# Diagonal blocks loaded group by group behind their stores, and the inverses of a scan's first groups stored in pieces of their own

## The chip, the core and the metric

The kernel runs on one core of one Trainium2 chip. The core has a matrix engine (PE, with its weight loads shown as PEld), a vector engine (DVE), a scalar engine (ACT), GpSimd (POOL), and SyncE (SP), which here does nothing but issue DMAs, in the order of its program. The metric is the time of one execution on the device in microseconds (us). A result is the median of several executions.

## What is computed

One layer of a hybrid encoder on x of 2048 rows and 1024 columns, in float32: RMSNorm, one combined input projection, then two groups of heads side by side, an output projection and the residual. One group is windowed attention (8 query heads, window 128). The other, with which the change is concerned, is a gated DeltaNet of 4 heads of width 128, scanned over the rows forward and backward. Cut to what matters, for one head and one direction, with the rows in chunks:

```python
g = jnp.cumsum(g, axis=-1)
decay = jnp.exp(jnp.where(incl, g[..., :, None] - g[..., None, :], -jnp.inf))
m = jnp.where(strict, jnp.einsum('bhncd,bhnsd->bhncs', k_beta, k) * decay, 0.0)
t_inv = triangular_solve(eye + m, eye, lower=True, unit_diagonal=True)
...
def step(state, inp):                      # one chunk after the other
    v_new = u_i - w_i @ state              # u, w = t_inv applied to v, k
    o = (q_i * exp(g_i)) @ state + a_i @ v_new
    state = state * exp(g_last) + k_dec.T @ v_new
```

Each chunk needs the inverse of a unit triangular matrix before its step of the scan, and the steps of a direction depend on each other through the state.

## The kernel before

The kernel uses chunks of 128 rows: 16 chunks a head and direction, in four groups of four (`c4` = 0 to 3). Phase A (`phase_a`) does norm, projections and attention. Phase B (`phase_b`) has four parts for each DeltaNet head `h`:

- `pre_front(h)`: for each group in the order FRONT = (1, 2, 0, 3) it loads k and q (L621), v (L623) and the decays (L631), multiplies k by k and q (tile `gh`, L661), forms the matrices `ma` for both directions (`d` = 0 and 1, L670), and stores the 128x128 matrices of the group to DRAM (`m_d<-ma`, L675: two DMAs a group, one a direction, 256 KB each, eight a head).
- `pre_back(h)`: it loads the 32x32 diagonal blocks out of `m_d`. A row of padding makes the four blocks of a matrix lie at equal distances, so that one strided DMA takes 64 of them, in pieces of 128 bytes: `L0` for direction 0 (L697) and the upper 64 partitions of `L` for direction 1 (L698), 256 KB each. DVE transposes the blocks of direction 0 into the lower half of `L` with one copy (L700). 31 steps on DVE (`tm` L705 and `X` L709, for all 128 blocks at once) then turn the identity in `X` (loaded in L699) into the inverses. One DMA stores all of `X` to DRAM (`x_d<-X`, L710, 512 KB). For each of four groups `hi`, two DMAs of 64 KB bring the inverses back in another layout (`xc<-x_d`, L718: the group `c4 = hi` of direction 0 and `c4 = 3 - hi` of direction 1), DVE transposes them (L719), POOL copies them into block matrices (`iv`, L724, L726 and L728, and `ma`, L745), and five rounds of matmuls (`pi`, L733) build the inverse of the whole 128x128 matrix.
- `scan(h)`: 16 steps, each for both directions: PE products `pk`, `py` and `po` (L773, L782, L784, L791, L800), scalings on ACT and DVE, and a load of k and q for the step (`kqc<-kq_d`, L771, four buffers a direction). Step `i` of the scan needs the inverses of group `hi = i // 4`, so `hi = 0` lets it begin.
- `post(h)`: norm and gate of the output (`jko` on ACT, `sso` on POOL, L829), stored as `mix_dn` (L843).

The calls stand in the order `pre_front(0)`, the attention half of the output projection (`out_sw`, tiles `pcs`, `xrs`), `pre_back(0)`, then `scan(h)`, `pre_front(h+1)`, `pre_back(h+1)` for `h` = 0, 1, 2, then `scan(3)` and the other half of the output projection (`out_dn`, tiles `pcd`). The engines do not run in that order. `set_order` (the planner) takes all instructions with their dependences and plans a start for each with costs of its own, forward and backward in turns, and then fixes the order on every engine by the plan. So work of head `h+1` is laid into the scan of head `h`. Two of its rules are used below: it counts an issue on SP as 500 ns, and it takes what waits for a DMA to be free 2400 ns plus bytes at 300 GB/s after the end of the issue:

```python
LAG = {"PE": 205, "DVE": 140, "Activation": 160, "Pool": 120, "SP": 2400}
...
            move[k] = a.ap[0][1] * size(a) * 4 / 300
```

Once planned, the order is fixed: an instruction that waits holds up all behind it on its engine, on SP too. A tile with one buffer (`L0`, `L`, `X`) can be written for the next head only when the last use of it for this head has ended; that also holds in the plan.

Of the kernel before, what the change touches and what calls it, by code (L numbers as in the profile page):

```python
# [7 lines left out]
F32 = mybir.dt.float32  # L8
# [7 lines left out]
P = 128  # L16
# [3 lines left out]
NCH = 16  # L20
# [496 lines left out]
def phase_b(ctx, tc, t, ident, consts, hp, mix_dn, mix_sw, kq_d, v_d, zdn_d, zsw_d, dp, out):  # L517
    nc = tc.nc
    V, A, G, T = nc.vector, nc.scalar, nc.gpsimd, nc.tensor
    dma = nc.sync.dma_start  # L520

    def pool(name, bufs=1, stack=ctx, **kw):
        return stack.enter_context(tc.tile_pool(name=name, bufs=bufs, reuse_waits="tile", **kw))
# [58 lines left out]
    qp = pool("qp", stack=pre_stack)  # L582
# [13 lines left out]
    def ma_tile(h, p):  # L596
        tag = f"ma{FREED[p] if h > 1 else p}"
        return hd[h % 2].tile([P, 4, 4, P], F32, tag=tag, name=f"ma{h}_{p}", bufs=1)

    def kv_tile(kind, h, n, name):  # L600
        p, slot = ((0, n), (1, n), (2, n) if n < 2 else (0, n - 2), (0, 2 + n) if n < 2 else (1, n - 2))[h]
        return (hd[p] if p < 2 else qp).tile([P, 4, P], F32, tag=f"{kind}{slot}", name=name, bufs=1)

    def pre_front(h):
        H = {}
        ssk = hp.tile([P, NCH], F32, tag="ssk", name=f"ssk{h}", bufs=1)
        nk = hp.tile([P, NCH], F32, tag="nk", name=f"nk{h}", bufs=1)
        bp = hp.tile([P, 2, NCH], F32, tag="bp", name=f"bp{h}")
        ssq = H["ssq"] = hp.tile([P, NCH], F32, tag="ssq", name=f"ssq{h}", bufs=3)
        ck = H["ck"] = hp.tile([P, 2, NCH], F32, tag="ck", name=f"ck{h}", bufs=3)  # L610
        ks = H["ks"] = {}
        vs = H["vs"] = {}
        mp = {}
        ma = H["ma"] = {}
        m_d = dp.tile([2, NCH, 4 * (32 * P + 32)], F32, tag="m_d", name=f"m_d{h}", bufs=2)
        x_d = dp.tile([2, NCH, P, 32], F32, tag="x_d", name=f"x_d{h}", bufs=2)
        for n, c4 in enumerate(FRONT):
            s4 = slice(4 * c4, 4 * c4 + 4)
            cs = slice(c4 * 512, (c4 + 1) * 512)
            kq = q1.tile([P, 2, 512], F32, tag="kq", name=f"kq{h}_{c4}", bufs=2)  # L620
            dma(kq, kq_d[h][:, :, cs])  # L621
            vt = q1.tile([P, 512], F32, tag="vt", name=f"vt{h}_{c4}", bufs=2)
            dma(vt, v_d[h][:, cs])  # L623
            gms = []
            for d in range(2):
                gm = q1.tile([P, 4, P], F32, tag="gm", name=f"dc{h}_{c4}_{d}", bufs=4)
                if h < NDEC:
                    dma(gm.rearrange("p c i -> p (c i)"), dec_d[h, d][c4])
                else:
                    src = gr_d[d].rearrange("(c h) i -> c h i", h=4)[s4, h]  # L630
                    dma(gm, src.partition_broadcast(P))  # L631
                    G.tensor_tensor(gm, gm, dmask[:, d : d + 1].to_broadcast([P, 4, P]), ALU.add)
                gms.append(gm)
                p = 3 - c4 if d else c4
                if p not in mp:
                    mp[p] = ma_tile(h, p)
                ma[d, c4] = mp[p][:, :, 1 - d :: 2]
            for j, ss in ((0, ssk), (1, ssq)):
                tr = ps_t.tile([P, 4, P], F32, tag="tr", name=f"tr{h}_{c4}_{j}")
                for c in range(4):  # L640
                    T.transpose(tr[:, c], kq[:, j, c * P : (c + 1) * P], ident)
                if j == 0:
                    ks[c4] = kv_tile("ks", h, n, f"ks{h}_{c4}")
                    A.activation(ks[c4], tr, AF.Copy)
                for c in range(4):
                    cc = 4 * c4 + c
                    src = ks[c4] if j == 0 else tr
                    jk = q1.tile([P, P], F32, tag="jk", name=f"jk{h}_{c4}_{j}_{c}", bufs=3)
                    A.activation(jk, src[:, c], AF.Square, accum_out=ss[:, cc : cc + 1])
            V.tensor_scalar(ssk[:, s4], ssk[:, s4], EPS, None, ALU.add)  # L650
            G.tensor_tensor(nk[:, s4], ssk[:, s4], pw[:, 0, :4], ALU.pow)
            V.reciprocal(ssk[:, s4], ssk[:, s4])
            V.tensor_tensor(
                bp[:, :, s4], beta[:, s4, h :: 4].rearrange("p c d -> p d c"),
                ssk[:, s4].unsqueeze(1).to_broadcast([P, 2, 4]), ALU.mult,
            )
            for c2 in range(2):
                gh = ps_g.tile([P, 2, 2, P], F32, tag="gh", name=f"gh{h}_{c4}_{c2}")
                for k in range(2):
                    c = 2 * c2 + k  # L660
                    T.matmul(  # L661
                        gh[:, k], kq[:, 0, c * P : (c + 1) * P], kq[:, :, c * P : (c + 1) * P], start=True, stop=True
                    )
                for k in range(2):
                    c = 2 * c2 + k
                    cc = 4 * c4 + c
                    for d in range(2):
                        if h >= NDEC:
                            A.activation(gms[d][:, c], gms[d][:, c], AF.Exp, bias=ngc[:, d, cc, h : h + 1])
                        V.scalar_tensor_tensor(  # L670
                            ma[d, c4][:, c], gh[:, k], bp[:, d, cc : cc + 1],
                            gms[d][:, c : c + 1].to_broadcast([P, 2, P]), ALU.mult, ALU.mult,
                        )
            for d in range(2):
                dma(m_d[d, s4, : P * P].rearrange("u (i j) -> i u j", j=P), ma[d, c4][:, :, 0])  # L675
            tr = ps_t.tile([P, 4, P], F32, tag="tr", name=f"trv{h}_{c4}")
            for c in range(4):
                T.transpose(tr[:, c], vt[:, c * P : (c + 1) * P], ident)
            vs[c4] = kv_tile("vs", h, n, f"vs{h}_{c4}")
            for c in range(4):  # L680
                cc = 4 * c4 + c
                A.activation(vs[c4][:, c], tr[:, c], AF.Copy, scale=nk[:, cc : cc + 1])
        for d in range(2):
            V.tensor_tensor(ck[:, d], bp[:, d], ekd[:, d, :, h], ALU.mult)

        H["solve"] = m_d, x_d, mp
        return H

    def pre_back(h, H):
        ma = H["ma"]  # L690
        m_d, x_d, mp = H["solve"]
        L0 = qp.tile([64, 32, 32], F32, tag="L0", name=f"L0{h}")
        L = qp.tile([P, 32, 32], F32, tag="L", name=f"L{h}")
        X = qp.tile([P, 32, 32], F32, tag="X", name=f"X{h}")
        lv = [m_d[d].rearrange("u (p y) -> (u p) y", p=4)[:, : 32 * P] for d in range(2)]
        lv = [a.rearrange("q (r x) -> q r x", x=P)[:, :, :32] for a in lv]
        dma(L0, lv[0])  # L697
        dma(L[64:128], lv[1])  # L698
        dma(X, t["eye32"].partition_broadcast(P))  # L699
        V.tensor_copy(L[0:64], L0.rearrange("p r c -> p c r"))  # L700
        for c in range(31):
            n = 31 - c
            tm = qp.tile([P, 256], F32, tag="tm", name=f"tm{h}_{c}")
            tv = tm[:, : n * (c + 1)].rearrange("p (r k) -> p r k", k=c + 1)
            XE.tensor_tensor(  # L705
                tv, L[:, c + 1 :, c : c + 1].to_broadcast([P, n, c + 1]),
                X[:, c : c + 1, 0 : c + 1].to_broadcast([P, n, c + 1]), ALU.mult,
            )
            XE.tensor_tensor(X[:, c + 1 :, 0 : c + 1], X[:, c + 1 :, 0 : c + 1], tv, ALU.subtract)  # L709
        dma(x_d.rearrange("d u (p r) c -> (d u p) (r c)", p=4), X.rearrange("p r c -> p (r c)"))  # L710
        for hi in range(4):
            e1, p2, e2, e3 = (z[hi % len(z)] for z in zts)
            m = mp[hi]
# [1 line left out]
            for d, c4 in ((0, hi), (1, 3 - hi)):  # L715
                xc = qp.tile([P, 4, 32], F32, tag="xc", name=f"xc{h}_{d}_{c4}", bufs=4)
                xt = qp.tile([P, 4, 32], F32, tag="xt", name=f"xt{h}_{d}_{c4}", bufs=4)
                dma(xc, x_d[d, 4 * c4 : 4 * c4 + 4].rearrange("u i c -> i u c"))  # L718
                V.transpose(xt.rearrange("p u c -> p (u c)"), xc.rearrange("p u c -> p (u c)"))  # L719
                x0[d], x1[d] = (xc, xt) if d == 0 else (xt, xc)  # L720
            g = qp.tile([P, 4, P], F32, tag="g", name=f"g{h}_{hi}", bufs=2)
# [111 lines left out]
    def post_rows(h, oa, so, c4):  # L833
# [9 lines left out]
        dma(mix_dn[h, :, c4 * 512 : (c4 + 1) * 512], zt)  # L843

    H = pre_front(0)
    with tc.using_default_side("right"):
        with ExitStack() as sw:
# [4 lines left out]
            )  # L852
        hd[1] = pool("hd1")
    pre_back(0, H)
    for h in range(3):
        scan(h, H)
        H = pre_front(h + 1)
        pre_back(h + 1, H)
# [365 lines left out]
```

## Time and profile before

| | |
|---|---|
| median of 3 runs | 1340.53 us (1336.61 to 1341.32) |
| profiled execution, its own time | 1339.74 us |
| span of its instructions | 1338.0 us, mean granted PE clock 0.979 |
| busy, of the span | PE 1258.0 us, DVE 885.6, ACT 711.3, POOL 484.4 |
| DMA | 201.16 MB, mean 150 GB/s |
| issues of `m_d` stores and `L` loads | 32 of 256 KB, 8 of 256 KB |
| issues of `x_d` stores and `xc` loads | 4 of 512 KB, 32 of 64 KB |

The span runs from the first to the last instruction of the profiled execution, and 1.7 us of that execution's time lie around it. In a row of the timeline stand start, duration, engine (SPq is SyncE's instruction queue), line, operation, output and input tiles, and, in brackets, how long the engine had been idle before and what ended the wait. A row of the stretches has their length, then the busy time of each engine with its count of instructions, the granted PE clock, the mean busy share of the 16 DMA engines, and GB/s. A row of the DMA issues ends with the size of one and the median time from issue to landing. The chain of waits is the chain of work that ended last, followed back from the last instruction.

### The profile page before, as it was taken

How to read it: one execution, taken by the hardware profiler on the slowest of the kernel's cores; microseconds unless marked ns; L12 is line 12 of the kernel's file. 1: busy time of each engine (PE TensorE's matmuls, PEld its weight loads, DVE VectorE, ACT ScalarE, POOL GpSimd, SP SyncE). 2: the span in 40 equal slices, each digit the busy share in tenths (PEclk: the TensorE clock that was granted, in tenths of full speed). 3: DMA queues.
4: the chain of work that ended last, by engine and by line, in shares of the span. 5: the costliest groups of instructions: out<-in, count | busy, mean ns of one | idle time of the engine just before them, and what ended most of it. 6: DMA issues, size and time to landing. Idle time of an engine off the chain costs nothing.

```text
span 1338.0 us, 22553 instructions
## 1 busy us (share of the span) xinstructions
PE 1258.0 (94%) x7162; PEld 1072.9 (80%) x7162; DVE 885.6 (66%) x2250; ACT 711.3 (53%) x2105; POOL 484.4 (36%) x868
## 2 busy tenths in 40 slices
PE   5999999999999999999999899998979879898998
PEld 4998878788998888888888687778868769788776
DVE  4423387773632399999987899666885877846433
ACT  5422264332433467666667877229868766466310
POOL 1223032100021235755786755228238155170000
PEclk8999999999999999999999999999979989989999
DMA  7442345244443533222334757968567274333776
GB/s 235 135 140 78 104 161 171 73 135 135 148 121 114 163 102 109 72 93 83 96 120 130 249 185 226 291 209 217 144 184 207 84 212 104 94 104 106 233 241 209
DMA packets 219686, 201.16 MB, mean 150 GB/s; under 512 B 48304, under 2 KB 170800, under 8 KB 219568
## 3 DMA queue, kind: packets, MB, share of 16 engines
q1 hardware_dynamic: 219568, 199.73, 48.8%
q8 instruction: 57, 0.93, 0.3%
q14 instruction: 61, 0.50, 0.1%
HBM read 134.59 MB, written 65.08 MB: 149 GB/s over the span
## 4 chain that ended last, share of the span: by engine, by line
PE 72%; DVE 9%; DMA 5%; ACT 5%; POOL 5%; issue 3%; SPq 0%; DVEq 0%; POOLq 0%; ACTq 0%
PE pf_c L186 6%; PE pf_c L187 6%; PE pf_c L188 5%; PE pf_z L186 4%; PE pf_z L187 4%; PE pf_z L188 4%; PE pi L733 4%; PE pt L360 2%; PE pq_q L197 2%; PE pq_q L199 2%; PE pq_q L198 2%; PE pcd L559 2%; PE pcd L560 2%; PE pcd L558 2%; PE pcs L558 2%
## 5 line engine op out<-in xcount | busy, mean ns | idle before, releaser
L237 DVE SCALAR_TENSOR_TENSOR acc<-pf_c,cw,acc 128x512 f32<-128x512 f32 (+1 forms) x192 | 140.0, 745 | 22.7 <-ACT acc L233 20.9
L186 PE MATMUL pf_c<-xhi,wh_c 128*128 128x512 f32 x384 | 149.3, 401 | 1.9 <-DVE acc L237 1.1
L187 PE MATMUL pf_c<-xlo,wh_c 128*128 128x512 f32 x384 | 150.4, 401 | 0.0
L188 PE MATMUL pf_c<-xhi,wl_c 128*128 128x512 f32 x384 | 148.4, 400 | 0.0
L186 PE MATMUL pf_z<-xhi,wh_z 128*128 128x512 f32 x256 | 91.6, 400 | 0.1
L355 POOL TENSOR_SCALAR pr<-pr,st 128x384 f32<-128x384 f32 (+1 forms) x128 | 83.5, 670 | 22.5 <-DVE st L353 19.0
L187 PE MATMUL pf_z<-xlo,wh_z 128*128 128x512 f32 x256 | 91.0, 397 | 0.0
L346 ACT ACTIVATE pr<-pr,st 128x384 f32<-128x384 f32 (+1 forms) x128 | 76.2, 598 | 27.3 <-DVE st L345 26.7
L188 PE MATMUL pf_z<-xhi,wl_z 128*128 128x512 f32 x256 | 90.3, 396 | 0.0
L186 PEld LDWEIGHTS pf_c<-xhi,wh_c 128*128 128x128 f32 x384 | 72.3, 189 | 17.5 <-DVE acc L237 1.9
L188 PEld LDWEIGHTS pf_c<-xhi,wl_c 128*128 128x128 f32 x384 | 72.0, 188 | 14.6
L187 PEld LDWEIGHTS pf_c<-xlo,wh_c 128*128 128x128 f32 x384 | 72.3, 188 | 13.9
L341 DVE CUSTOM_DVE_ANT_0 pr<-s,mask,sink 128x384 f32<-128x384 f32 (+1 forms) x128 | 72.6, 594 | 6.0 <-PE pt L360 2.5
L360 PE MATMUL pt<-ident,pr 128*128 128x128 f32 x368 | 72.8, 276 | 3.3 <-ACT q L323 1.4
L364 ACT ACTIVATE ph<-pt 128x512 fp32r<-128x512 f32 x92 | 53.4, 594 | 40.2 <-PE pt L360 37.3
L365 DVE TENSOR_TENSOR pl<-pt,ph 128x512 fp32r<-128x512 f32 x92 | 62.5, 684 | 9.1 <-ACT ph L364 7.9
L670 DVE SCALAR_TENSOR_TENSOR ma<-gh,bp,dc 128x256 f32<-128x256 f32 x128 | 56.1, 476 | 17.7 <-PE gh L661 10.0
L787 ACT ACTIVATE yk<-py,ck 128x128 f32<-128x128 f32 x120 | 44.0, 367 | 40.4 <-PE py L782 39.1
L360 PEld LDWEIGHTS pt<-ident,pr 128*128 128x128 f32 x368 | 48.6, 141 | 19.2 <-POOL pr L355 4.8
L178 DVE TENSOR_TENSOR wl_c<-ws_c,wh_c 128x512 fp32r<-128x512 f32 x48 | 36.6, 765 | 37.0 <-ACT wh_c L177 24.7
L197 PE MATMUL pq_q<-wh_q,xhi 128*128 128x256 f32 x256 | 58.5, 284 | 0.8 <-ACT sgq L256 0.8
L561 DVE TENSOR_TENSOR xrd<-xrd,pcd 128x512 f32<-128x512 f32 x32 | 20.9, 684 | 55.5 <-PE pcd L560 55.5
(250 smaller groups left out, 3769.9 us busy)
## 6 DMA issues: line engine op xcount, KB each, us to landing
kqc<-kq_d SPq DMA_DIRECT2D x120, 128.0 KB, 2.5
ws_c<-wt SPq DMA_DIRECT2D x48, 256.0 KB, 3.5
xr<-x SPq DMA_DIRECT2D x16, 512.0 KB, 6.0
ws_z<-wt SPq DMA_DIRECT2D x32, 256.0 KB, 3.4
kq<-kq_d SPq DMA_DIRECT2D x16, 512.0 KB, 4.9
xrs<-x SPq DMA_DIRECT2D x32, 256.0 KB, 3.4
part<-xrs SPq DMA_DIRECT2D x32, 256.0 KB, 3.4
m_d<-ma SPq DMA_DIRECT2D x32, 256.0 KB, 4.9
```

The source lines that it names most:

```text
L186: T.matmul(ps, hi[:, k, cs], xhi[b][:, k], start=(k == 0), stop=False)
L187: T.matmul(ps, hi[:, k, cs], xlo[b][:, k], start=False, stop=False)
L188: T.matmul(ps, lo[:, k, cs], xhi[b][:, k], start=False, stop=(k == KC - 1))
L197: T.matmul(ps[:, :n], xh, hi[:, k, :n], start=(k == 0), stop=False)
L237: V.scalar_tensor_tensor(av, ps[:, lo:], cw[:, i, k : k + 1], av, ALU.mult, ALU.add)
L341: V.tensor_tensor_reduce(pr[j][:, :n], ps[:, :n], mask[:, lo * P : hi * P], 1.0, sink[:, hh : hh + 1], ALU.add, ALU.max, accum_out=mx[:, j ...
L346: A.activation(pr[j][:, :n], pr[j][:, :n], AF.Exp, bias=nm[:, j : j + 1], accum_out=den[:, j : j + 1])
L355: G.tensor_scalar(pr[j][:, :n], pr[j][:, :n], den[:, j : j + 1], 1.0, ALU.mult, ALU.mult)
L360: T.transpose(pt[:, j], pr[j][:, (kb - lo) * P : (kb - lo + 1) * P], ident)
L365: V.tensor_tensor(pl, ptf, ph.bitcast(F32), ALU.subtract)
L558: T.matmul(ps, mh[:, k], wh[:, k, ns], start=(k == 0), stop=False)
L670: V.scalar_tensor_tensor(ma[d, c4][:, c], gh[:, k], bp[:, d, cc : cc + 1], gms[d][:, c : c + 1].to_broadcast([P, 2, P]), ALU.mult, ALU.mult,)
```

## The change

`L0` and `L` are now created in `pre_front`, and `m_d` becomes a tile of one group. Right behind the two stores of a group, two DMAs load that group's diagonal blocks, 16 partitions each (64 KB): eight loads a head in place of two. `x_d` is split into three tiles, and the store of `X` into three DMAs: partitions 0 to 15 (direction 0, group 0), 112 to 127 (direction 1, group 3), which together are all that `hi = 0` reads, and then the other 96. The loads `xc` read from the tile that holds their group. The arithmetic is the same.

```diff
@@ pre_front
-        m_d = dp.tile([2, NCH, 4 * (32 * P + 32)], F32, tag="m_d", name=f"m_d{h}", bufs=2)
-        x_d = dp.tile([2, NCH, P, 32], F32, tag="x_d", name=f"x_d{h}", bufs=2)
+        L0 = qp.tile([64, 32, 32], F32, tag="L0", name=f"L0{h}")
+        L = qp.tile([P, 32, 32], F32, tag="L", name=f"L{h}")
+        x_d = [dp.tile([4 * n, P, 32], F32, tag=f"x_d{j}", name=f"x_d{h}_{j}", bufs=2) for j, n in enumerate((1, 1, 6))]
         for n, c4 in enumerate(FRONT):
...
+            m_d = dp.tile([2, 4, 4 * (32 * P + 32)], F32, tag=f"m_d{n}", name=f"m_d{h}_{c4}", bufs=2)
             for d in range(2):
-                dma(m_d[d, s4, : P * P].rearrange("u (i j) -> i u j", j=P), ma[d, c4][:, :, 0])
+                dma(m_d[d, :, : P * P].rearrange("u (i j) -> i u j", j=P), ma[d, c4][:, :, 0])
+            for d in range(2):
+                lv = m_d[d].rearrange("u (p y) -> (u p) y", p=4)[:, : 32 * P]
+                lo = 64 * d + 16 * c4
+                dma((L if d else L0)[lo : lo + 16], lv.rearrange("q (r x) -> q r x", x=P)[:, :, :32])
@@ pre_back
-        L0 = qp.tile([64, 32, 32], F32, tag="L0", name=f"L0{h}")
-        L = qp.tile([P, 32, 32], F32, tag="L", name=f"L{h}")
         X = qp.tile([P, 32, 32], F32, tag="X", name=f"X{h}")
-        lv = [m_d[d].rearrange("u (p y) -> (u p) y", p=4)[:, : 32 * P] for d in range(2)]
-        lv = [a.rearrange("q (r x) -> q r x", x=P)[:, :, :32] for a in lv]
-        dma(L0, lv[0])
-        dma(L[64:128], lv[1])
...
-        dma(x_d.rearrange("d u (p r) c -> (d u p) (r c)", p=4), X.rearrange("p r c -> p (r c)"))
+        for a, lo, hi in zip(x_d, (0, 112, 16), (16, 128, 112)):
+            dma(a.rearrange("u (p r) c -> (u p) (r c)", p=4), X[lo:hi].rearrange("p r c -> p (r c)"))
...
-                dma(xc, x_d[d, 4 * c4 : 4 * c4 + 4].rearrange("u i c -> i u c"))
+                lo = 4 * (3 * d + c4 - 1 + d)
+                dma(xc, (x_d[2][lo : lo + 4] if hi else x_d[d]).rearrange("u i c -> i u c"))
```

More of the change, by code (lines that the diff above doesn't have):

```diff
@@ L684, in pre_front @@
             V.tensor_tensor(ck[:, d], bp[:, d], ekd[:, d, :, h], ALU.mult)
-        H["solve"] = m_d, x_d, mp
+        H["solve"] = L0, L, x_d, mp
         return H
@@ L690, in pre_back @@
         ma = H["ma"]
-        m_d, x_d, mp = H["solve"]
-        L0 = qp.tile([64, 32, 32], F32, tag="L0", name=f"L0{h}")
-        L = qp.tile([P, 32, 32], F32, tag="L", name=f"L{h}")
+        L0, L, x_d, mp = H["solve"]
         X = qp.tile([P, 32, 32], F32, tag="X", name=f"X{h}")
-        lv = [m_d[d].rearrange("u (p y) -> (u p) y", p=4)[:, : 32 * P] for d in range(2)]
-        lv = [a.rearrange("q (r x) -> q r x", x=P)[:, :, :32] for a in lv]
-        dma(L0, lv[0])
-        dma(L[64:128], lv[1])
         dma(X, t["eye32"].partition_broadcast(P))
```

## The prediction, as put on record before the result

> **What bounds the kernel now.** I read the page first: the busy shares and the chain of waits by engine.
>
> ```profile
> span 1338.0 us, 22553 instructions
> PE 1258.0 (94%) x7162; PEld 1072.9 (80%) x7162; DVE 885.6 (66%) x2250; ACT 711.3 (53%) x2105; POOL 484.4 (36%) x868
> PE 72%; DVE 9%; DMA 5%; ACT 5%; POOL 5%; issue 3%; SPq 0%; DVEq 0%; POOLq 0%; ACTq 0%
> ```
>
> PE is busy for 1258.0 of 1338.0 us and carries 72% of the chain. So the change, which touches no matmul, can win only where PE stands idle, and only in the part where diagonal blocks are solved. The stretches of that part say how much there is:
>
> ```profile
> 855.00:890.00 35.00, 33.14 (x143) 26.29 (x142) 30.62 (x80) 3.17 (x5) 0.00 (x0) 1.00 0.87 292
> 890.00:905.00 15.00, 11.56 (x64) 9.71 (x63) 4.80 (x14) 7.18 (x31) 9.39 (x31) 0.89 0.50 133
> 905.00:950.00 45.00, 42.44 (x320) 38.93 (x319) 30.04 (x95) 41.49 (x179) 32.26 (x66) 1.00 0.84 216
> 950.00:990.00 40.00, 35.14 (x234) 30.49 (x234) 38.13 (x141) 26.13 (x117) 5.32 (x5) 0.91 0.44 125
> 990.00:1010.00 20.00, 15.27 (x86) 13.10 (x86) 11.14 (x33) 16.70 (x72) 15.16 (x35) 0.74 0.97 261
> 1010.00:1055.00 45.00, 43.69 (x349) 40.84 (x349) 32.88 (x107) 36.20 (x138) 26.93 (x61) 1.00 0.52 139
> 1055.00:1090.00 35.00, 26.00 (x152) 21.93 (x152) 29.61 (x106) 21.60 (x107) 9.22 (x8) 0.90 0.60 179
> 1090.00:1120.00 30.00, 25.27 (x176) 22.24 (x175) 16.47 (x48) 20.97 (x80) 23.61 (x69) 0.94 0.63 154
> 1120.00:1160.00 40.00, 35.05 (x271) 32.48 (x270) 35.91 (x129) 24.82 (x94) 9.58 (x20) 0.98 0.23 64
> 1160.00:1176.00 16.00, 13.01 (x74) 10.89 (x73) 8.90 (x32) 5.80 (x28) 5.44 (x19) 0.82 0.59 168
> 1176.00:1240.00 64.00, 59.16 (x455) 55.30 (x453) 35.88 (x111) 44.12 (x156) 23.09 (x66) 0.98 0.36 102
> ```
>
> Length less the first busy number, added up, gives 45.3 us of idle PE in 385 us. Where a solve ends and a scan begins (990, 1090 and 1160) PE idles and its clock is granted at 0.74, 0.94 and 0.82; before 990 and 1160 DVE is nearly full (38.13 of 40 and 35.91 of 40), because it solves one head and scans another.
>
> The edits are on two hand-overs through DRAM. Third view: the timeline of SP, with the DVE copy that begins each solve, for heads 1 and 2, then 3.
>
> ```profile
> 937.39 0.59 SPq L675 DMA_DIRECT2D m_d<-ma  x1
> 943.09 0.60 SPq L697 DMA_DIRECT2D L<-m_d  x1
> 948.19 1.06 DVE L700 COPY L<-L 64x1024 f32<-64x1024 f32 x1
> 1017.48 0.50 SPq L675 DMA_DIRECT2D m_d<-ma  x1
> 1027.94 1.62 DVE L700 COPY L<-L 64x1024 f32<-64x1024 f32 x1
> 1104.88 0.50 SPq L675 DMA_DIRECT2D m_d<-ma  x1
> 1111.13 0.61 SPq L697 DMA_DIRECT2D L<-m_d  x1
> 1116.45 1.06 DVE L700 COPY L<-L 64x1024 f32<-64x1024 f32 x1
> ```
>
> From a head's last store to the copy pass 10.8, 10.5 and 11.6 us. In heads 1 and 3 the rows of the first load split this: 5.7 and 6.3 us to its issue, 5.1 and 5.3 from there to the copy. The second hand-over, x_d, by the same view, heads 0 to 3, with POOL's first copy for head 3 (for the others below):
>
> ```profile
> 888.13 0.33 SPq L710 DMA_DIRECT2D x_d<-X  x1
> 890.80 0.92 SPq L718 DMA_DIRECT2D xc<-x_d  x2
> 986.79 0.33 SPq L710 DMA_DIRECT2D x_d<-X  x1
> 992.73 0.37 SPq L718 DMA_DIRECT2D xc<-x_d  x1
> 1082.76 0.46 SPq L710 DMA_DIRECT2D x_d<-X  x1
> 1089.13 0.92 SPq L718 DMA_DIRECT2D xc<-x_d  x2
> 1160.03 0.34 SPq L710 DMA_DIRECT2D x_d<-X  x1
> 1163.72 2.72 SPq L771 DMA_DIRECT2D kqc<-kq_d  x2
> 1166.55 2.19 SPq L718 DMA_DIRECT2D xc<-x_d  x4
> 1168.73 0.61 POOL L724 COPY iv<-xc 32x128 f32<-32x128 f32 x2 [10.61 <-DMA xc<-x_d]
> ```
>
> From store to first load pass 2.7, 5.9, 6.4 and 6.5 us. In head 3 the queue did it: two kqc loads, ahead of xc in SP's order, stood from 1163.72.
>
> **The change part by part.** Prices come from the landings on the page:
>
> ```profile
> q_d<-sgq SPq DMA_DIRECT2D x32, 128.0 KB, 1.8
> L<-m_d SPq DMA_DIRECT2D x8, 256.0 KB, 4.5
> xc<-x_d SPq DMA_DIRECT2D x32, 64.0 KB, 2.9
> ```
>
> *Loads of L.* Removed behind a head's last store: two loads of 256 KB. Added: two of 64 KB there (the other six lie earlier, beside the front's own work). The number of 128-byte pieces stays. No load of this shape is in the trace; the nearest row is xc, 64 KB in 128-byte pieces, 2.9 us. With one more issue ahead (I take 0.45; xc issues took 0.37 to 0.46 apiece above) the copy can begin 3.4 us after the first issue, in place of 5.1 and 5.3: 1.8 us won a head. Bounds: landing as slowly as L itself, 4.5, wins 0.2; as fast as q_d, 1.8, wins 2.9. I take 1.8. What of it is on the path:
> - Head 0: PE has out_sw matmuls (33.14 of 35 us busy). I take 0; if that cover is gone, at most the 3.4 idle of 890 to 905.
> - Head 1: a solve that starts earlier moves DVE work out of a stretch that is full (38.13 of 40) into one that is one third free (30.04 of 45): 1.8 x 0.33 = 0.6.
> - Head 2: DVE is 27% free from 1010 (32.88 of 45) and 85% full later; between 0.5 and 1.8 I take 1.0.
> - Head 3: the load itself is on the chain, whose piece follows, and DVE is half idle ahead of it (16.47 of 30): all 1.8.
>
> ```profile
> 1111.84 4.66 DMA L<-m_d
> ```
>
> Together 3.4 us.
>
> *Store of X.* One store becomes three, and the first xc waits for the first alone. Issue to xc was 2.7 us in head 0, for the whole store. For a 64 KB store I take that 2.7 for all heads; three issues of 0.33 and q_d's 1.8 give 2.8, about the same. Won: 3.2, 3.7 and 3.8 us in heads 1 to 3, nothing in head 0. Other end: in head 1 the DMA engines are 0.97 busy, and the store may take as long as now, 0 won. What POOL does with it:
>
> ```profile
> 996.55 0.61 POOL L724 COPY iv<-xc 32x128 f32<-32x128 f32 x2 [1.89 <-DMA xc<-x_d]
> 1094.31 0.61 POOL L724 COPY iv<-xc 32x128 f32<-32x128 f32 x2
> ```
>
> - Head 1: POOL waits 1.89 us for xc, with other work before it: 1.9.
> - Head 2: iv starts at 1094.31, 5.2 us after xc's issue, so POOL's order held it, not xc. The planner may put it ahead; of 3.7 I take 2.5.
> - Head 3: POOL idles 10.61 us until xc. PE idles 3.0 in 1160 to 1176: of 3.8 I take 3.0.
>
> Together 7.4 us. The rest of X lands later than its first parts, but `hi` = 1 is needed only four scan steps on.
>
> *What is added.* Landings of the m_d store, least, median, most:
>
> ```profile
> DMA to landing us min/median/max: 2.4/4.9/7.5
> ```
>
> There are 24 more L loads and 8 more stores, 32 x 0.4 = 13 us of issue spread over some 375. More important, **each group's loads wait on SP for the group's stores**, with everything behind them: kq, dc and vt loads of the next group, kqc loads of the running scan. The planner expects a store 0.5 + 2.4 + 0.87 = 3.8 us after its start; the row says 4.9. So SP stands 1.1 us a group where the plan has it moving, 16 groups, 17.6 us. Kqc has four buffers a direction and kq and dc loads run a group ahead, which hides most; I charge 1.5 us, for the crowded front of head 2 (DMA share 0.97). The ends are nothing (an added wait can't win) and all of it (rival 2). The early loads of head 3 must also wait until head 2's solve leaves `L`; they come free at the same moment as the x_d store, for which SP waits today as well, so I add nothing.
>
> Sum: -3.4 - 7.4 + 1.5 = -9.3. The profiled execution took 1339.7 (span and 1.7 around it), which gives 1330.4; it lies 0.8 below the median of the runs, so I say **1331**.
>
> At the x_d store a rule speaks against this. The Trainium skill, "DMA: Bandwidth & Descriptors", section "Anatomy of one DMA — SWDGE (gpsimd) path", has a fixed cost of about 2.0 us a DMA plus bytes at 436 GB/s, mostly the receipt of the write. By it 64 KB in place of 512 KB wins 1.0 us, and 64 KB in place of 256 KB wins 0.45; with the shares of the path used above, my estimate from the Trainium skill is some 3 us won before the added waits. The trace disagrees for L (4.5 us for 256 KB against 2.9 for xc); the fit is one for DMAs issued by GpSimd, and here SP issues them all.
>
> **The rivals.**
> 1. *The landing is set by what is queued, not by size.* For: a 513 KB store lands in 2.9 us, so 5.9 and 6.4 were other transfers' doing.
>
> ```profile
> kq_d<-acc SPq DMA_DIRECT2D x8, 513.0 KB, 2.9
> ```
>
> Then a store wins 2.9 - 1.8 = 1.1 us a head, 3.3 in all, of which I count two thirds, 2.2; L keeps 3.4; less 1.5 is -4.1: 1336. Against: in head 3 it was SP's order. The Trainium skill's fit, above, would also end in this case.
> 2. *SP's queue becomes the bound*, the slower side. Place: the front of each head, behind the L loads. If all 17.6 us reach the path and head 2's four groups, whose DMA is crowded, stand another 0.5 each (2.0; a landing took up to 7.5), it costs 19.6 against the 10.8 won: 1348.5, or 1349 by the median. It decides from 10.8 us, 0.7 a group. For: kq is double-buffered only. Against: the chain holds SPq at 0%.
> 3. *The loads don't come right behind the stores.* The planner places them by planned times; behind kqc and xc, as in head 3 today, the last pair wins nothing: -7.4 + 1.5, 1334.6 with the median.
>
> **How the numbers follow.** Forecast 0.45, rivals 0.25, 0.22 and 0.08. With both ends of the L landing and all of the x_d gains (8.7 for L, 10.7 for x_d, nothing added) the best is -19.4, 1321; the plan is made anew for all engines, so I go to 1318. Above, most of rival 2 belongs in: 1350. A measurement of this kernel tells about 0.5% from no change, here 6.7 us: below 1333.8 or above 1347.2. Faster takes 0.42 of the forecast and 0.06 from rivals 1 and 3; slower takes 0.18 from rival 2 and 0.02 from poor plans; the rest is 0.32.
>
> **What would show it.** L right: from the last m_d store to L700 some 9 us in place of 10.5 to 11.6. X right: x_d to first xc under 3 us in heads 1 to 3, and no 10.61 us wait of POOL in head 3. Rival 2: SP waiting for m_d landings ahead of kq or kqc, and PE idle in 905 to 950 and 1010 to 1055, where it has 2.6 and 1.3 now. The forecast is wrong if the new plan puts other work at the hand-overs than the old one, or if a solve, given its blocks earlier, ends no earlier because DVE is full.

## The result, and the profile after

The changed kernel took **1352.82 us** (median of 5 runs, 1348.03 to 1355.22) against 1341.05 before (5 runs): ratio 1.0092, interval 1.0071 to 1.0113. It is slower by 0.9%, where 1331 was forecast. The profiled execution took 1352.82 with a span of 1351.0 us, 13.0 longer than before. Medians and ratios here and below leave out three disturbed executions: one of f_head0 (6837.80 us), one of d_before_2340 (1771.26) and one of the kernel before beside x_only (1946.63).

The page of the changed kernel, busy shares and chain by engine:

```profile
span 1351.0 us, 22579 instructions
PE 1264.5 (94%) x7162; PEld 1075.5 (80%) x7162; DVE 888.4 (66%) x2250; ACT 714.2 (53%) x2105; POOL 482.8 (36%) x868
PE 74%; DVE 9%; ACT 6%; DMA 4%; POOL 3%; issue 3%; SPq 0%; DVEq 0%; ACTq 0%; POOLq 0%
```

The compute engines run the same instructions, and SP's queue is still at 0% of the chain. Of the 13.0 us, PE is busy for 6.5 (1264.5 for 1258.0, with the same 7162 matmuls) and idle for the other 6.5. Where that happens shows when the hand-overs are followed in time. The timeline of head 0, first the kernel before (its other rows stand in the prediction), then the changed one:

```profile
785.51 0.37 SPq L675 DMA_DIRECT2D m_d<-ma  x1
838.87 0.67 SPq L675 DMA_DIRECT2D m_d<-ma  x1
853.48 1.12 DVE L700 COPY L<-L 64x1024 f32<-64x1024 f32 x1
```

```profile
790.79 0.37 SPq L677 DMA_DIRECT2D m_d<-ma  x1
843.88 1.13 SPq L681 DMA_DIRECT2D L<-m_d  x2
853.71 0.43 SPq L677 DMA_DIRECT2D m_d<-ma  x1
866.74 1.19 SPq L681 DMA_DIRECT2D L<-m_d  x2
872.46 1.09 DVE L700 COPY L<-L 64x1024 f32<-64x1024 f32 x1
903.76 1.26 SPq L711 DMA_DIRECT2D x_d<-X  x3
```

Head 0's x_d store goes from 888.13 to 903.76, 15.6 us later, and the four parts add up: the first m_d store is 5.3 later, the front from first to last store takes 62.9 us for 53.4 (+9.6), last store to copy 18.8 for 14.6 (+4.1), the solve 31.3 for 34.7 (-3.4). The early loads don't come early here: the first pair is issued at 843.88, 50 us behind its stores, because `L0` and `L` lie in memory that attention uses until then (its last store, `mix_sw<-ot`, is issued at 839.88). And the last pair stands 13 us behind the last store.

From there on nothing more is lost; head 3's x_d store is 15.7 us later than before, and the end 13.0. X's stores and the first xc of heads 1 to 3, and head 1's L in the changed kernel:

```profile
910.55 0.36 SPq L677 DMA_DIRECT2D m_d<-ma  x1
948.36 0.59 SPq L677 DMA_DIRECT2D m_d<-ma  x1
950.61 2.17 SPq L681 DMA_DIRECT2D L<-m_d  x2
954.68 1.06 DVE L700 COPY L<-L 64x1024 f32<-64x1024 f32 x1
1001.12 0.45 SPq L711 DMA_DIRECT2D x_d<-X  x1
1006.46 0.42 SPq L720 DMA_DIRECT2D xc<-x_d  x1
1098.58 0.97 SPq L711 DMA_DIRECT2D x_d<-X  x2
1104.01 0.59 SPq L720 DMA_DIRECT2D xc<-x_d  x1
1175.70 1.47 SPq L711 DMA_DIRECT2D x_d<-X  x3
1180.29 0.38 SPq L720 DMA_DIRECT2D xc<-x_d  x1
```

From one x_d store to the next pass 97.4, 97.5 and 77.1 us; before it was 98.7, 96.0 and 77.3. So the hand-overs did get shorter (last store to copy 6.3, 7.2 and 8.7 us in heads 1 to 3, for 10.8, 10.5 and 11.6; x_d to xc 5.3, 5.4 and 4.6 for 5.9, 6.4 and 6.5), and yet a head takes about as long as before. In head 1 the first m_d store stands 6.8 us behind head 0's x_d store in place of 18.7 (first store before at 906.82, row below), but its front, first to last store, takes 37.8 us where it took 30.6, and its solve, copy to x_d store, 46.4 where it took 38.6.

```profile
906.82 0.42 SPq L675 DMA_DIRECT2D m_d<-ma  x1
```

The stretches of the changed kernel around head 0's hand-over show where PE lost it:

```profile
855.00:890.00 35.00, 30.28 (x130) 23.95 (x129) 20.66 (x47) 7.91 (x25) 2.30 (x2) 0.95 0.93 291
890.00:905.00 15.00, 10.81 (x48) 8.27 (x47) 12.89 (x37) 2.90 (x17) 1.03 (x1) 0.90 0.33 107
905.00:950.00 45.00, 38.46 (x242) 34.06 (x243) 24.30 (x74) 34.64 (x143) 35.05 (x88) 0.84 0.82 212
```

PE idles 4.7, 4.2 and 6.5 us where it idled 1.9, 3.4 and 2.6, and its clock is granted at 0.95, 0.90 and 0.84 where it was 1.00, 0.89 and 1.00. How much of the 6.5 us of longer busy time is that clock was not tried.

### The profile page after: what moved, and what is told of

Its sections match the earlier page's. It is cut to its first block, busy times and chain, and to the rows that moved or that the text cites. A ratio compares the mean times of both kernels' runs of the same rounds, so it can differ in the third digit from the quotient of the medians.

```text
span 1351.0 us, 22579 instructions
## 1 busy us (share of the span) xinstructions
PE 1264.5 (94%) x7162; PEld 1075.5 (80%) x7162; DVE 888.4 (66%) x2250; ACT 714.2 (53%) x2105; POOL 482.8 (36%) x868
## 4 chain that ended last, share of the span: by engine, by line
PE 74%; DVE 9%; ACT 6%; DMA 4%; POOL 3%; issue 3%; SPq 0%; DVEq 0%; ACTq 0%; POOLq 0%
PE pf_c L186 6%; PE pf_c L187 6%; PE pf_c L188 6%; PE pi L735 5%; PE pf_z L186 4%; PE pf_z L187 4%; PE pf_z L188 4%; PE pt L360 2%; PE pq_q L197 2%; PE pcd L559 2%; PE pcd L560 2%; PE pcd L558 2%; PE pq_q L198 2%; PE pq_q L199 2%; PE gh L662 2%
```

## The experiments

Three theories stood after the result. H: head 0's loads. S: SP stands waiting for m_d stores (rival 2). P: the planner, given any other input, draws another order, and orders differ.

**One part alone, head 0 as before, and no edit at all.** x_only has the edit of `x_d`, `X` and `xc` alone, l_only that of `m_d`, `L0` and `L` alone. h0_old is the changed kernel with (excerpt, comments added)

```diff
+            for d in range(2 if h else 0):   # the loads by group
...
+        if h == 0:                           # in pre_back: L0, L and the two old loads
```

and re_lag is the kernel before with

```diff
-LAG = {"PE": 205, "DVE": 140, "Activation": 160, "Pool": 120, "SP": 2400}
+LAG = {"PE": 205, "DVE": 140, "Activation": 160, "Pool": 120, "SP": 2420}
```

> The kernel before with the store of X in three pieces alone; the planner makes a new order. Theory H (the loss is head 0's early loads of L, which can't begin before attention gives up the memory): no early loads here, so 1333 to 1341. Theory S (SP stands waiting for m_d stores, rival 2 of the prediction): also 1333 to 1341, for nothing waits for m_d ahead of its old place. Theory P (any edit makes the planner draw another order, and orders differ by some 10 us whatever the edit is): anywhere in 1334 to 1352, with the four head periods and phase A changed alike.

> The changed kernel with X stored by one DMA again: the loads of L by group alone. H: as slow as the changed kernel, 1350 to 1356, with the store-to-copy time of head 0 near 18 us. S: the same, but with the fronts of all four heads 5 to 9 us longer than before. P: anywhere in 1338 to 1356.

> The changed kernel, but head 0 loads its blocks by two DMAs in pre_back as before; heads 1 to 3 and the store of X as changed. H: the loss is gone, 1330 to 1341, and head 0's x_d store comes near 888 us in place of 904. S: heads 1 to 3 still pay for their waits, 1346 to 1352. P: anywhere in 1334 to 1352.

> The kernel before with the same instructions; only the planner's time from a DMA's issue to its landing is 2420 ns in place of 2400, so that it draws another order. H and S: within 0.3% of before, 1337 to 1345. P: clearly off, by 5 us or more, with the same number of instructions and bytes.

| kernel | median us | ratio to before | interval |
|---|---|---|---|
| x_only | 1344.08 | 1.0029 | 1.0012 to 1.0045 |
| l_only | 1348.34 | 1.0081 | 1.0052 to 1.0110 |
| h0_old | 1344.38 | 1.0028 | 1.0010 to 1.0046 |
| re_lag | 1357.74 | 1.0135 | 1.0117 to 1.0154 |

re_lag decides most. It has the instructions and bytes of the kernel before, and a number that exists only in the planner moved by 20 ns; it is slower by 1.35%, more than the change. Its timeline, too, has lost the time by head 0's x_d store:

```profile
873.82 1.10 DVE L700 COPY L<-L 64x1024 f32<-64x1024 f32 x1 [0.17 <-DMA L<-m_d]
909.50 0.32 SPq L710 DMA_DIRECT2D x_d<-X  x1
```

Its copy is 20.3 us later than in the kernel before and its x_d store 21.4, with two loads and one store, as ever. It lost it earlier, though: its first m_d store, at 808.95, is 23.4 us later than before, that of the changed kernel 5.3. H and S both had re_lag within 0.3%. The other three lie in the ranges of P and in none of H or S, but they go H's way: the two that spare head 0 the early loads lose 0.3%, l_only 0.8%, and h0_old has its x_d store back at 891.36. So these four don't rule out that head 0's loads have a part in it.

**The order held still.** To take the draw away, the planner was replaced by a list: each engine's order in the kernel before, written out, so that PE, DVE, ACT and POOL keep it exactly and SP differs only by the moved DMAs.

```diff
-    end, begin, queue = best
+    queue = {e: [per[e][j] for j in fixed[e]] for e in ENGINES if e != "SP"}
...
+    queue["SP"] = sorted(sp, key=key.get)
```

> Both hand-overs changed, in the old order: the planner is left out, every instruction of PE, DVE, ACT and POOL stands in the order of the kernel before, and so does SP apart from the moved DMAs. X's three stores stand where the one stood; heads 1 to 3 load L by group, the first three groups behind the next group's stores, the last where the old loads stood; head 0 loads as before. If the prediction's terms were right and only the new order ate them: -10.8 us less what fixed orders can't use, 1329 to 1336. If the hand-overs win nothing on the chip even so: 1338 to 1344. If the added DMAs themselves cost: over 1345.

> As f_both, but X stored by one DMA, so the loads of L alone. By the prediction's terms -3.4 us: 1336 to 1339. If DVE is too full to use earlier blocks: 1339 to 1343. A cost of the early loads would show as 1344 or more.

> As f_both, but in heads 1 to 3 each group's loads stand directly behind its later store in SP's order, so that SP must wait for the store to land. Rival 2 (SP becomes the bound): twelve groups stand some 5 us each, and the time rises by 10 us or more over f_both. The prediction's charge for such waits, 1.5 us: within 3 us of f_both, the loads behind being issued well ahead of their use.

> As f_both, but head 0's blocks come by eight loads of 64 KB as well, at the place of the old two (they can't stand earlier, the memory being attention's). Six issues more, ahead of which the solve can't begin: 0 to 3 us over f_both. If head 0's eight loads are by themselves what made the changed kernel slow: 8 us or more over f_both.

| kernel | median us | ratio to before | interval |
|---|---|---|---|
| f_both | 1340.65 | 1.0005 | 0.9986 to 1.0024 |
| f_l | 1342.21 | 1.0015 | 0.9998 to 1.0032 |
| f_wait | 1360.18 | 1.0142 | 1.0102 to 1.0182 |
| f_head0 | 1343.01 | 1.0009 | 0.9987 to 1.0032 |

In the old order the edit neither loses nor wins, within some 3 us (the interval of f_both). f_head0 clears the eight loads of head 0 at the place of the old two. f_both contradicts the prediction's prices: heads 1 and 2 in its timeline, and its rows of DMA issues.

```profile
940.83 0.59 SPq L679 DMA_DIRECT2D m_d<-ma  x1
949.87 1.06 DVE L709 COPY L<-L 64x1024 f32<-64x1024 f32 x1
988.68 1.26 SPq L720 DMA_DIRECT2D x_d<-X  x3
993.47 0.51 SPq L729 DMA_DIRECT2D xc<-x_d  x1
1020.67 0.51 SPq L679 DMA_DIRECT2D m_d<-ma  x1
1031.42 1.20 DVE L709 COPY L<-L 64x1024 f32<-64x1024 f32 x1
1085.60 1.38 SPq L720 DMA_DIRECT2D x_d<-X  x3
1091.11 1.11 SPq L729 DMA_DIRECT2D xc<-x_d  x2
```

```profile
L<-m_d SPq DMA_DIRECT2D x24, 64.0 KB, 4.4
x_d<-X SPq DMA_DIRECT2D x8, 64.0 KB, 3.2
```

Store to copy takes 9.0 and 10.8 us (before 10.8 and 10.5), x_d to xc 4.8 and 5.5 (5.9 and 6.4); in head 3 they take 11.3 and 7.1 (11.6 and 6.5). A load of L of 64 KB lands in 4.4 us, where I took 2.9 and the 256 KB load had 4.5. And the fronts took longer, which uses up what the loads won: from first to last m_d store heads 1 to 3 take 32.4, 34.3 and 37.5 us, where they took 30.6, 33.0 and 36.9. Whether the added issues on SP did that was not tried.

f_wait shows that the danger of rival 2 is real when the loads stand directly behind the stores. Its SP, and the changed kernel's, by the view of SP's waits (total, times, longest; the first from 900 to 1130 us, the second over the span):

```profile
SPq L683 <- DMA m_d<-ma: 38.7, 13, 4.8
```

```profile
SPq L681 <- DMA m_d<-ma: 1.2, 1, 1.2
```

38.7 us of standing cost 1.4%. In the changed kernel SP stood 1.2 us in all: the planner had put other DMAs between. So S isn't what made it slow. (The 38.7 us came to 13 stands of 3.0 us on the mean, and about half of them, 19.5 us, reached the time: f_wait against f_both.)

**The reverse, and other draws.** r_order has the old instructions in the changed kernel's order. a_new is the changed kernel, h0_new is h0_old and b_new the kernel before, each with other planner numbers: 2300 ns to a landing in all three, and for an issue 505 ns in h0_new and 490 in b_new, so that they aren't a clean pair.

> The reverse of f_both: the instructions of the kernel before (two loads of L a head, one store of X), in the order of the changed kernel on all five engines; the two loads stand where the last two of the eight stood, the one store where the first of three stood. If the new order is what made the changed kernel slow: 1347 to 1358. If the added and split DMAs are: 1337 to 1344.

> The changed kernel, with the planner's time to a landing at 2300 ns in place of 2400, so that it draws another order. If one draw made the loss: off the changed kernel's 1352.8 by 5 us or more, most likely 1343 to 1350. If the change itself carries the loss whatever the order: 1350 to 1356.

> h0_old with 2300 ns to a landing and 505 ns for an issue in the planner, another draw of its order. If the early loads in heads 1 to 3 are worth something once the order suits them: 1331 to 1338, which would beat both kernels. If draws scatter by themselves: 1337 to 1350.

> The kernel before with 2300 ns to a landing and 490 ns for an issue in the planner: a second draw of its order beside re_lag, with its instructions untouched, and the control for h0_new. If draws scatter: anywhere in 1335 to 1352, and not with re_lag's 1357.7. If a shorter landing time in the planner is wrong for the chip, as landings of 4.9 us say: over 1345.

| kernel | median us | ratio to before | interval |
|---|---|---|---|
| r_order | 1353.43 | 1.0087 | 1.0054 to 1.0121 |
| a_new | 1337.75 | 0.9981 | 0.9958 to 1.0003 |
| h0_new | 1338.47 | 0.9987 | 0.9967 to 1.0008 |
| b_new | 1342.14 | 1.0016 | 0.9996 to 1.0036 |

r_order, without a single DMA of the change, is as slow as the changed kernel (1.0087 and 1.0092), and its timeline is the changed kernel's:

```profile
791.54 0.37 SPq L675 DMA_DIRECT2D m_d<-ma  x1
851.88 0.43 SPq L675 DMA_DIRECT2D m_d<-ma  x1
872.81 1.09 DVE L700 COPY L<-L 64x1024 f32<-64x1024 f32 x1
906.24 0.32 SPq L710 DMA_DIRECT2D x_d<-X  x1
947.40 0.59 SPq L675 DMA_DIRECT2D m_d<-ma  x1
954.88 1.07 DVE L700 COPY L<-L 64x1024 f32<-64x1024 f32 x1
```

Together with f_both this is a two by two: old order, 1340.5 and 1340.65 with old and new DMAs; new order, 1353.43 and 1352.82. (f_both loads head 0 as before; with its eight loads, f_head0, it is 1343.01.) Within the intervals the order makes all of the difference. It also made part of the shorter hand-overs, as the last two rows show for head 1 with the old loads. In us, heads 1, 2 and 3:

| kernel | order | DMAs | last m_d store to copy | x_d to first xc |
|---|---|---|---|---|
| before | old | old | 10.8, 10.5, 11.6 | 5.9, 6.4, 6.5 |
| f_both | old | new | 9.0, 10.8, 11.3 | 4.8, 5.5, 7.1 |
| r_order | new | old | 7.5, 10.6, 8.9 | 5.1, 4.9, 3.4 |
| changed | new | new | 6.3, 7.2, 8.7 | 5.3, 5.4, 4.6 |

With the order held, the loads by group are worth between 0.3 us lost and 3.5 won a head, and the store in pieces between 1.2 lost and 1.1 won.

What the new order did ahead of that is seen on out_sw's matmuls (tile pcs on PE: length, busy time, count), which feed PE while head 0 is solved, before and after:

```profile
775.00:853.00 78.00, 46.74 (x169) 1.00 0.74 221
```

```profile
775.00:853.00 78.00, 50.58 (x180) 1.00 0.68 212
```

11 more of them ran ahead of and between head 0's front, which came later; PE then idled at the hand-over. That this is what makes an order slow isn't shown, and a_new speaks against it. It is the changed kernel with one planner number different and loses nothing, yet it has still more of these matmuls there, and its x_d store of head 0 is 12.1 us later than before:

```profile
775.00:853.00 78.00, 52.18 (x183) 1.00 0.69 210
```

```profile
900.25 1.26 SPq L711 DMA_DIRECT2D x_d<-X  x3
1159.02 1.31 SPq L711 DMA_DIRECT2D x_d<-X  x3
```

By head 3's x_d store (1160.03 before) a_new has won all of that back, which the changed kernel doesn't (1175.70). So a late head 0 isn't enough for a slow kernel; what follows has to stay slow as well. No draw clearly beats the kernel before.

**Pairs of draws**, at planner numbers chosen beforehand, the same for both kernels:

> The kernel before, another draw of its order: 2340 ns to a landing in the planner. Theory P alone (the edit has no effect of its own, only the draw): anywhere in 1335 to 1358, on either side of the changed kernel's draw at 2340.

> The changed kernel at 2340 ns. P alone: anywhere in 1335 to 1358, on either side of its partner. If the edit is worth the 10 us of the prediction under a planner that may use it: below its partner in each pair, by 5 us or more on the mean. If it costs by itself: above in each.

> The kernel before at 2460 ns. As at 2340: anywhere in 1335 to 1358 by P.

> The changed kernel at 2460 ns: on either side of its partner by P, 5 us or more below it if the edit has the worth predicted, above if it costs.

| ns to a landing | kernel before | changed kernel |
|---|---|---|
| 2340 | 1350.85, 1.0074 (1.0047 to 1.0100) | 1353.85, 1.0102 (1.0074 to 1.0129) |
| 2460 | 1349.40, 1.0070 (1.0049 to 1.0092) | 1350.73, 1.0075 (1.0048 to 1.0103) |

Within a pair the intervals overlap. Other draws of the kernel before give 1357.7, 1342.1, 1350.9 and 1349.4, mean 1350.0; four of the changed one 1352.8, 1337.8, 1353.9 and 1350.7, mean 1348.8. The spread within either (16 us) is over ten times the difference of the means (1.2). An effect of the edit of its own isn't seen, though with four draws of each kernel an effect of several us, either way, isn't ruled out. The kernel before is a good draw, 10 us under the mean of its four siblings, so an edit after which the planner draws anew can lose that much without a cost of its own.

The draws may not be pure chance. At 2300 ns all three kernels lie within 0.2% of the kernel before, at 2340 to 2460 all five lie 0.7 to 1.35% above it. Whether 2300 suits this kernel or three draws were lucky isn't shown.

## Why the prediction was wrong, point by point

- **The step that failed** is the new order, which was put at nothing. All terms were laid into the old order, and the sum's last step, "the plan is made anew for all engines, so I go to 1318", let the new plan widen the range downward only. The runs put the new order at +13 us (r_order, +0.87%) in place of nothing, and that alone takes the time above 1350. The rest of the way from 1331 is the gains: -9.3 us in the sum, nothing in the old order (f_both, 1.0005).
- **The loads of L**, "1.8 us won a head", rested on xc's 2.9 us for the landing. L's 64 KB landed in 4.4 us in f_both, near the upper bound that I had (4.5, which wins 0.2). Won in the old order: 1.8, -0.3 and 0.2 in heads 1 to 3, while the fronts took 1.8, 1.3 and 0.6 longer. The sign for L, "some 9 us in place of 10.5 to 11.6", came true in the changed kernel (6.3, 7.2 and 8.7), but r_order has 7.5, 10.6 and 8.9 with the old loads, and the time didn't follow.
- **The store of X**, "x_d to first xc under 3 us": 4.8, 5.5 and 7.1 in f_both, 5.3, 5.4 and 4.6 in the changed kernel. Rival 1, that the landing goes by what else is queued, had this right for heads 1 and 2, where the changed kernel's three pieces landed in 3.0 to 4.8 us. In head 3 they landed in 2.2 to 3.6, and SP's order came on top, as before: two kqc loads and another stand ahead of xc. POOL's wait for xc in head 3, which was to vanish, is there:

```profile
1183.86 0.61 POOL L726 COPY iv<-xc 32x128 f32<-32x128 f32 x2 [11.86 <-DMA xc<-x_d]
```

- **The added waits**: charged at 1.5 us, they were 1.2 us of SP's time, as the planner had laid other DMAs between store and load. Rival 2 gave 1348.5, near the measured time, for a reason that did not act: that was luck. So is it that its 19.6 us resemble f_wait's loss of 19.7: it had 16 groups at 1.1 us and four of them 0.5 longer, all of it on the path, and f_wait had 13 stands of 3.0 us, half of it on the path.
- **Head 0** was costed at nothing because out_sw's matmuls hide it. In the old order they do (f_head0, 1.0009). I had not seen that the loads of head 0 can't be early, `qp` lying where attention's pools were. At the old place that did no harm; whether a plan made around these eight loads is worse for them isn't shown.
- **What bounds the kernel** held: PE at 94%. Half of what was lost is idle PE, at the hand-over of head 0's solve above all, and half is the same matmuls taking longer.

Left open: which of the planner's choices makes one order 10 us better than the next. For the changed kernel the place of the loss is shown; a_new, late at the same place and not slow, shows that it isn't the whole of the matter.

## What to carry to other kernels

Where a heuristic planner draws the whole order, run an edit that changes nothing (one planner constant) before you believe an edit of a per cent: here five draws of one kernel lay between 1340 and 1358 us. To learn what an edit itself is worth, freeze the old order and put only the new instructions into it; to learn what the order is worth, put the old instructions into the new one. And put a wait for a store into an in-order DMA queue only where the store has landed: directly behind it cost 1.4%, some places later nothing.

## What the runs showed of the hardware

For L a transfer's landing hardly went by its size. The changed kernel's rows of DMA issues, and the DMA share (next to last column) of stretches in which its x_d stores of heads 0 and 2 are in flight:

```profile
L<-m_d SPq DMA_DIRECT2D x32, 64.0 KB, 4.7
x_d<-X SPq DMA_DIRECT2D x8, 64.0 KB, 2.6
x_d<-X SPq DMA_DIRECT2D x4, 384.0 KB, 4.1
```

```profile
903.00:908.00 5.00, 1.96 (x7) 1.48 (x7) 2.72 (x11) 1.75 (x6) 1.03 (x1) 0.50 0.58 132
1098.00:1104.00 6.00, 4.23 (x27) 2.97 (x25) 5.61 (x20) 3.55 (x23) 2.28 (x2) 1.00 0.86 246
```

A quarter of L took 4.7 us where the whole of a direction had taken 4.5. For the x_d stores both size and traffic show: the medians are 2.6 us for 64 KB and 4.1 for 384 KB, and the three stores of a head landed in 1.9 to 3.1 us at a DMA share of 0.58 (head 0) and in 3.8 to 4.8 at 0.86 (head 2):

```profile
DMA to landing us min/median/max: 1.9/2.1/3.1
```

```profile
DMA to landing us min/median/max: 3.8/4.2/4.8
```

Heads 3 and 1 lie between: 2.2 to 3.6 us at a share of 0.78, 3.0 to 4.6 at 0.86. So the price rose with what else was in flight, in four cases of one profile; no run changed the traffic alone. The Trainium skill, "DMA: Bandwidth & Descriptors", section "Latency and other measured facts", says that the latency of memory behind a DMA's fixed cost grows with the load on it; the trace agrees in the direction. Whether the 128-byte pieces are what keeps L's small loads slow was not tried.
